# A ninth pair by seven products, one set of weight sums, and a fourth raw place in a hybrid encoder layer

## The chip, the core and the metric

The kernel runs on one core of a Trainium2 chip. A core has five engines with their own instruction queues: TensorE (PE, matrix products; PEld is its loading of the stationary operand), VectorE (DVE), ScalarE (ACT), GpSimd (POOL) and SyncE (SP), which here only issues the loads of weights. Each works through its queue in the order in which the program put the instructions there, and waits at an instruction until the semaphores that it names have come. The metric is the device time in microseconds of one execution of the program; the number given for a kernel is the median of several.

## The reference

One encoder layer on 256 frames of 4096 channels, all in float32. Cut to what matters:

```
h = layer_norm(x)                                   # 256 x 4096
proj = h @ w_in                                     # 4096 x 24592: sixteen thousand columns of
                                                    # q, k, v, g twice, 16 forget logits, 8192 gate logits
y_r = group_norm(retention(rotary(q_r), rotary(k_r), v_r)) * silu(g_r)
y_f = forgetting_attention(q_f, k_f, v_f, f_logit + b_forget) * silu(g_f)
gates = sigmoid(gate_logit + b_gate)
merged = gates[0] * (y_r @ w_branch_ret) + gates[1] * (y_f @ w_branch_fox)
out = layer_norm(2**0.25 * h + merged @ w_out)
```

The product `h @ w_in` is most of the work, and the change is in it alone.

## The kernel before

**Products in three parts.** Each float32 operand is split into a high part (a cast by ACT) and a low part (the operand minus the high part, by DVE), and one product is three matmuls: high by high, high by low, low by high (`three`, L199 to L202). `split_into` (L154) is the pair of instructions: line 155 is ACT's cast, line 156 DVE's subtraction. The rows of the profile name the tiles `whi` and `wlo` for weights, `hTh` and `hTl` for the transposed normalised input.

**Groups of sixteen pairs.** Most columns of `w_in` are worked off in groups of 1024 columns: four groups of gates and then sixteen of projections, twenty in all (L889 to L892). A group sums over 4096 input channels in sixteen *pairs* of 256 channels, in the order of `PAIRS` (L32): 8, 0, 9, 1, and so on to 15, 7. A pair is a 2 by 2 block product: two halves of 128 frames, two blocks of 128 channels, two halves of 512 columns.

**Plain pairs and seven pairs.** A plain pair does the eight block products in the obvious way, 24 matmuls of 128x512. A pair named in `SEVEN` (8 to 15, so eight of sixteen) does seven products of sums (the Winograd form of Strassen's scheme), 21 matmuls. For that it needs sums of blocks of the input, made once ahead of the first group (`make_sops`, L363, tiles `soh` and `sol`), and sums of blocks of the weights, made anew for every pair (`u_split`, L183 to L197): `ta` and `tb` in float32 by DVE, then cast and subtracted into the tile `tset`. `tset` holds t1 and t3 (from `ta`) and t2 and t4 (from `tb`). In what follows S is a seven pair, P a plain one, and S15 is the pair number 15.

**Banks.** A group's eight products are accumulated in the eight banks of PSUM: 1, 2, 6, 5 in the tiles `acc`, 3, 7, 4, x in the tiles `ps` (`pair_pe`, L219). A plain pair adds to 2, 3, 4 and x, a seven pair to all but x. Since all eight are in use, the next group can begin with a bank only when ACT has copied the old one out (`proj_evac`, L391, tiles `ev`): 1, 6, 5, 7 after the last seven pair, 2, 3, 4, x after the last pair. `combine` (L405) then makes the four output blocks out of the eight copies with DVE, eight additions for a projection and eleven for gates, one behind each of the next steps (`late_step`).

**What sets the order.** The places: raw weights come by DMA into `wraw` (1 MB for a pair), three places in turn (`RAW = 3`, `load_more`, L923, loads the next one when the splitting of an old one has been issued). The split weights of a pair go into one of two sets of tiles, the sets alternating from pair to pair (`slots_for`, L928); `tset` alternates between two places of its own, t0 and t1, which lie in the tiles `yb0` and `yb1` of the room that the input had. The order of the instructions in each engine's queue is then set by a scheduler in the tile framework, which moves instructions of neighbouring pairs past each other; nothing is moved while the kernel runs.

Of the kernel before, what the change touches and what calls it, by code (L numbers as in the profile page):

```python
# [8 lines left out]
F32 = mybir.dt.float32  # L9
F32R = mybir.dt.float32r  # L10
# [18 lines left out]
FRONT = 2  # L29
SEVEN = tuple(range(8, 16))  # L30
GATE0, GATE1 = 7, 15
PAIRS = tuple(p for i in range(8) for p in (8 + i, i))  # L32


@with_exitstack
def hybrid_kernel(
# [27 lines left out]
    def bcast(ap1, n0, n):  # L64
        return ap1[n0:n0 + n].rearrange("(o n) -> o n", o=1).to_broadcast([P, n])


    xt = []
    for t in range(T):
        xt.append(big.tile([P, D], F32, name=f"x{t}", tag=f"yb{t}"))  # L70
    for t in range(T):
# [52 lines left out]

    def add_pair(wname, hi, lo, sops, order, evac):

        holder = {}
        last = lambda some: max(i for i, p in enumerate(order) if (p in sops) == some)
        final = dict(x=last(False), **{k: last(True) for k in "1567"})
        for i, p in enumerate(order):  # L130
            loads.append(dict(n=4 * NC, srcs=[take(wname, 4 * P * NC)], users=1))
            units.append(dict(kind="p", ld=loads[-1], p=p, seven=p in sops, hi=hi, lo=lo, sops=sops, g=i,
                              ng=len(order), evac=evac, h=holder, drain=False, pre=None, final=final))

    def u_load(ld):
        raw = wp.tile([P, 4 * NC], F32, name="wraw", tag="wraw", bufs=RAW)
        w = ld["srcs"][0].shape[0] // P
        for i, src in enumerate(ld["srcs"]):
            nc.sync.dma_start(raw[:, i * w:(i + 1) * w], src.rearrange("(p f) -> p f", p=P))
        ld["raw"] = raw  # L140
# [18 lines left out]
    def u_split(u):  # L159
# [30 lines left out]
        split_into(st[1][0][:, :NC], st[1][1][:, :NC], B[3])  # L190
        ts = big.tile([P, 2, 2, 2, NC], F32R, name="tset", tag="yb0" if u["slots"][2] == "t0" else "yb1")
        for i, t_ in enumerate((ta, tb)):
# [26 lines left out]
    def pair_pe(u):  # L219
# [143 lines left out]
    def make_sops(hi, lo, pairs_, sops):  # L363
        sh = big.tile([P, len(pairs_), 4, P], F32R, name="soh", tag="yb2")
        sl = big.tile([P, len(pairs_), 4, P], F32R, name="sol", tag="yb3")
        for n_, p in enumerate(pairs_):
            sops[p] = (sh[:, n_], sl[:, n_])
        yield
        for n_, p in enumerate(pairs_):
# [8 lines left out]
            nc.vector.tensor_tensor(o[:, 0, :], a12, o[:, 2, :], op=ALU.add)  # L378
            split_into(sh[:, n_], sl[:, n_], o)
            yield  # L380
# [102 lines left out]
    def retention():  # L483
# [3 lines left out]
        yr["h"] = big.tile([P, 16, S], F32R, name="yrh", tag="yb0")  # L487
        yr["l"] = big.tile([P, 16, S], F32R, name="yrl", tag="yb1")

# [313 lines left out]
    def out_chunk(j):  # L803
# [3 lines left out]
        def pre():  # L807
            if not z:
                for t in range(T):
                    z[t] = big.tile([P, D], F32, name=f"z{t}", tag=f"yb{t}")  # L810
                bg.append(post_rows())
# [111 lines left out]
    def load_more():  # L923
        while state["loaded"] < min(len(loads), state["done"] + RAW):
            u_load(loads[state["loaded"]])
            state["loaded"] += 1

    def slots_for(i, s_):  # L928
        u = units[i]
        if u["kind"] == "p":  # L930
            cands = [("r0", "r1") if (i - first_pair) % 2 else ("a0", "a1")]
            if u["seven"]:
                state["t"] = state.get("t", 0)
                cands = [c + ("t" + str(state["t"] % 2),) for c in cands]
        else:
            cands = u["cands"]
        for c in cands:
            if all(q not in user or last_step[user[q]] < s_ for q in c):
                if u["kind"] == "p" and u["seven"]:
                    state["t"] += 1  # L940
                return c
        return None
# [52 lines left out]
    for s_, (i, tiles) in enumerate(steps):  # L995
# [140 lines left out]
```

## Time and profile before

| | |
|---|---|
| time, median of 3 runs | 2832.47 us (2830.31 to 2833.13) |
| the profiled execution | 2837.31 us, span 2835.5 us |
| PE busy | 2791.1 us, 98% |
| DVE busy | 2308.0 us, 81% |
| ACT busy | 1569.0 us, 55% |
| mean granted TensorE clock | 0.996 |

The four groups of gates lie at about 115 to 457 us of the span, the sixteen groups of projections at 457 to 1763 us, the attention branches, merge and output projection behind them. A busy time is the union of an engine's instructions. Durations of neighbours on one engine overlap by about a tenth of a microsecond, so the pace of an engine is read from start to start, not from the durations. The granted clock of 1.00 in a row is TensorE at 2.4 GHz, 0.50 would be 1.2 GHz throughout.

### The profile page before, as it was taken

What the parts mean: (1) busy time and instruction counts of PE and PEld (TensorE: products, weight loads), DVE (VectorE), ACT (ScalarE), POOL (GpSimd) and SP (SyncE); (2) the same over time, 40 slices, a digit from 0 to 9 for tenths busy, and PEclk for the clock granted to TensorE, in tenths of its full rate; (3) what the DMA queues carried; (4) which work ended last, traced back from release to release, by engine and by line L of the source; (5) the groups of instructions that cost most, each with busy time, mean ns of one, the idle gap of its engine ahead of it and who ended that gap; (6) DMA issues with size and microseconds to landing.
All of it is one profiled execution on the core that took longest, in us unless ns stands there. A gap on an engine that the chain in (4) does not pass through costs nothing. (4 is left out here: it accounts for less than half of the span.)

```text
span 2835.5 us, 34653 instructions
## 1 busy us (share of the span) xinstructions
PE 2791.1 (98%) x12666; PEld 2312.5 (82%) x12666; DVE 2308.0 (81%) x2988; ACT 1569.0 (55%) x2170; POOL 170.1 (6%) x302
## 2 busy tenths in 40 slices
PE   7999999999999999999999999999999999999998
PEld 5788888888888888888888888888898888888886
DVE  7889998999999999899999998977675666656666
ACT  5555666565566565655555565444664444444443
POOL 1000000000000000000000000212220000000000
PEclk9999999999999999999999999999999999999999
DMA  6456666656666655555665656866676556666564
GB/s 221 182 211 227 231 224 217 215 223 217 221 223 223 220 217 216 212 217 218 230 222 208 234 208 236 283 222 208 197 232 220 207 210 218 224 216 230 211 231 171
DMA packets 128157, 620.28 MB, mean 219 GB/s; under 512 B 15804, under 2 KB 16076, under 8 KB 87020
## 3 DMA queue, kind: packets, MB, share of 16 engines
q1 hardware_dynamic: 105552, 543.47, 53.2%
q0 software_dynamic: 21856, 72.49, 8.3%
q8 instruction: 99, 1.62, 0.2%
q10 hardware_dynamic: 576, 2.10, 0.2%
q14 instruction: 74, 0.60, 0.1%
HBM read 588.54 MB, written 29.46 MB: 218 GB/s over the span
## 5 line engine op out<-in xcount | busy, mean ns | idle before, releaser
L155 ACT CAST whi<-wraw 128x1024 fp32r<-128x1024 f32 (+1 forms) x640 | 594.5, 946 | 408.8 <-PE ps L202 221.5
L156 DVE TENSOR_TENSOR wpart<-wraw,wpart 128x512 fp32r<-128x512 f32 (+2 forms) x790 | 521.5, 669 | 316.0 <-ACT wpart L155 314.0
L155 ACT CAST wpart<-wraw 128x512 fp32r<-128x512 f32 (+2 forms) x790 | 475.4, 606 | 524.8 <-DVE wpart L156 312.9
L156 DVE TENSOR_TENSOR wlo<-wraw,whi 128x1024 fp32r<-128x1024 f32 (+1 forms) x640 | 684.4, 1088 | 23.2 <-ACT whi L155 23.0
L201 PE MATMUL ps<-wlo,hTh 128*128 128x512 f32 x960 | 374.5, 390 | 0.6 <-DVE wlo L156 0.6
L202 PE MATMUL ps<-whi,hTl 128*128 128x512 f32 x960 | 374.4, 390 | 0.0
L200 PE MATMUL ps<-whi,hTh 128*128 128x512 f32 x960 | 328.3, 390 | 0.0
L186 DVE TENSOR_TENSOR ta<-wraw 128x1024 f32<-128x1024 f32 x160 | 195.9, 1225 | 113.2 <-DMA wraw<-in_w_in 112.5
L201 PE MATMUL acc<-wlo,hTh 128*128 128x512 f32 x640 | 246.9, 390 | 4.2 <-DVE wlo L156 4.1
L200 PE MATMUL acc<-whi,hTh 128*128 128x512 f32 x640 | 246.3, 390 | 1.5 <-ACT whi L155 1.4
L202 PE MATMUL acc<-whi,hTl 128*128 128x512 f32 x640 | 246.1, 389 | 0.0
L155 ACT CAST tset<-tb 128x1024 fp32r<-128x1024 f32 x160 | 168.5, 1053 | 129.1 <-DVE tb L189 128.7
L155 ACT CAST tset<-ta 128x1024 fp32r<-128x1024 f32 x160 | 168.1, 1051 | 119.8 <-DVE ta L186 119.6
L201 PE MATMUL acc<-wpart,hTh 128*128 128x512 f32 (+2 forms) x568 | 212.1, 377 | 4.1 <-DVE wpart L156 4.1
L201 PEld LDWEIGHTS ps<-wlo,hTh 128*128 128x128 f32 x960 | 180.6, 188 | 38.6 <-DVE wlo L156 1.0
L200 PEld LDWEIGHTS ps<-whi,hTh 128*128 128x128 f32 x960 | 180.7, 188 | 37.7
L202 PEld LDWEIGHTS ps<-whi,hTl 128*128 128x128 f32 x960 | 180.7, 188 | 37.6
L202 PE MATMUL acc<-wpart,hTl 128*128 128x512 f32 (+2 forms) x568 | 208.6, 371 | 0.6 <-DVE rstd L96 0.6
L156 DVE TENSOR_TENSOR tset<-tb,tset 128x1024 fp32r<-128x1024 f32 x160 | 195.5, 1222 | 1.1 <-ACT tset L155 1.1
L156 DVE TENSOR_TENSOR tset<-ta,tset 128x1024 fp32r<-128x1024 f32 x160 | 195.4, 1221 | 0.0
L201 PE MATMUL acc<-wpart,mTh 128*128 128x512 f32 x500 | 194.6, 389 | 0.0
L202 PE MATMUL acc<-wpart,mTl 128*128 128x512 f32 x500 | 194.5, 389 | 0.0
(257 smaller groups left out, 4853.8 us busy)
## 6 DMA issues: line engine op xcount, KB each, us to landing
wraw<-in_w_in SPq DMA_DIRECT2D x320, 1024.0 KB, 4.9
wraw<-in_w_out SPq DMA_DIRECT2D x128, 512.0 KB, 4.1
wraw<-in_w_in SPq DMA_DIRECT2D x112, 512.0 KB, 4.5
wraw<-in_w_branch_ret SPq DMA_DIRECT2D x64, 512.0 KB, 4.2
wraw<-in_w_branch_fox SPq DMA_DIRECT2D x64, 512.0 KB, 4.2
proj_d<-ev POOLq DMA_DIRECT2D x64, 256.0 KB, 2.7
g<-gates_d POOLq DMA_DIRECT2D x16, 512.0 KB, 5.7
wraw<-in_w_in SPq DMA_DIRECT2D x16, 272.0 KB, 4.3
```

The costliest lines, as they stand in the source:

```text
L155: c = nc.scalar.copy(hi, src)
L156: nc.vector.tensor_tensor(lo, src, hi.bitcast(F32), op=ALU.subtract)
L186: nc.vector.tensor_tensor(ta, B[0][:, None, :].to_broadcast([P, 2, NC]), raw[:, NC:3 * NC].rearrange("p (a n) -> p a n", a=2), op=ALU.add)
L200: nc.tensor.matmul(o, lhsT=a[0], rhs=w[0], start=first, stop=False)
L201: nc.tensor.matmul(o, lhsT=a[0], rhs=w[1], start=False, stop=False)
L202: return nc.tensor.matmul(o, lhsT=a[1], rhs=w[0], start=False, stop=last)
```

## The change

Nine of the sixteen pairs go by seven products in the sixteen groups of projections (7 to 15); in the four groups of gates pair 7 stays plain. The order of pairs becomes 8, 0, 9, 1, 10, 2, 11, 3, 12, 4, 13, 5, 14, 7, 15, 6, so that in a projection S14, S7 and S15 follow one another. There is one `tset` instead of two. Its second room and a part of the room of the sums of the input become: a fourth place for raw weights, `wraw3`, which takes every fourth pair's load, and the ninth pair's sums of the input (`sope`). The loads may run four pairs ahead. The products of a seven pair and the copies of the banks come in another order, those with t1 and t3 first. The tile `x1`, `yrl` and `z1`, which lie in the same room later or earlier, are kept in two halves.

```diff
-SEVEN = tuple(range(8, 16))
+SEVEN = tuple(range(7, 16))
-PAIRS = tuple(p for i in range(8) for p in (8 + i, i))
+PAIRS = (8, 0, 9, 1, 10, 2, 11, 3, 12, 4, 13, 5, 14, 7, 15, 6)
...
     def u_load(ld):
-        raw = wp.tile([P, 4 * NC], F32, name="wraw", tag="wraw", bufs=RAW)
+        if ld.get("pair", 0) % 4 == 3:
+            raw = scr["raw"]
+        else:
+            raw = wp.tile([P, 4 * NC], F32, name="wraw", tag="wraw", bufs=RAW)
...
-        ts = big.tile([P, 2, 2, 2, NC], F32R, name="tset", tag="yb0" if u["slots"][2] == "t0" else "yb1")
+        ts = scr["t"]
...
-            work_ = [("1", blk(0, 0), f["b11"]), ("6", so(2), f["t2"]), ("5", so(1), f["t1"]), ("7", so(3), f["t3"]),
-                     ("2", blk(0, 1), f["b21"]), ("3", so(0), f["b22"]), ("4", blk(1, 1), f["t4"])]
+            work_ = [("5", so(1), f["t1"]), ("7", so(3), f["t3"]), ("6", so(2), f["t2"]), ("1", blk(0, 0), f["b11"]),
+                     ("4", blk(1, 1), f["t4"]), ("2", blk(0, 1), f["b21"]), ("3", so(0), f["b22"])]
...
     def make_sops(hi, lo, pairs_, sops):
-        sh = big.tile([P, len(pairs_), 4, P], F32R, name="soh", tag="yb2")
-        sl = big.tile([P, len(pairs_), 4, P], F32R, name="sol", tag="yb3")
+        so = [big.tile([P, 4, 2, 4, P], F32R, name="sop", tag=f"yb{2 + i}") for i in range(2)]
+        end = big.tile([P, 2, 2, 4, P], F32R, name="sope", tag="yb1b")
+        scr["t"] = big.tile([P, 2, 2, 2, NC], F32R, name="tset", tag="yb0")
+        scr["raw"] = big.tile([P, 4 * NC], F32, name="wraw3", tag="yb1a")
...
     for i in range((GATE1 - GATE0) // 2):
-        add_pair("w_in", hTh, hTl, sops, PAIRS, proj_evac(gates[GATE0 + 2 * i][0], True))
+        add_pair("w_in", hTh, hTl, sops, PAIRS, proj_evac(gates[GATE0 + 2 * i][0], True), 7)
...
     def load_more():
-        while state["loaded"] < min(len(loads), state["done"] + RAW):
+        while state["loaded"] < len(loads):
+            pair = loads[state["loaded"]].get("pair", 0)
+            if state["loaded"] >= state["done"] + RAW + (pair >= RAW and "raw" in scr) or pair == RAW and "raw" not in scr:
+                break
             u_load(loads[state["loaded"]])
...
-            u["evac"](u["h"]["m"], "1657")
+            u["evac"](u["h"]["m"], "5761")
         if u["g"] == u["ng"] - 1:
             if u["kind"] == "p":
-                u["evac"](u["h"]["m"], "234x")
+                u["evac"](u["h"]["m"], "423x")
```

The change moves instructions most at the end of each group of projections. The sixteen ends have two orders that alternate, eight of the one, seven of the other; the last end is followed by other work. Below is what stands there. In the changed file the cast is line 182, the subtraction 183, the matmuls of `three` 227 to 229, the bank copies 430.

ACT's queue at the end of the sixth group of projections, before. `acc_6865` to `ps_6872` are the banks 1, 2, 6, 5, 3, 7, 4, x in this order, `tset_7452` and `whi_7441`, `whi_7439` belong to the next group's first pair:

```order
L155 CAST tset_7452<-ta_7445 128x1024
L155 CAST whi_7402<-wraw_7299 128x1024
L400 COPY ev_7431<-acc_6865 128x512
L400 COPY ev_7433<-acc_6867 128x512
L400 COPY ev_7435<-acc_6868 128x512
L400 COPY ev_7437<-ps_6870 128x512
L155 CAST whi_7441<-wraw_7333 128x512
L155 CAST whi_7439<-wraw_7333 128x1024
L155 CAST tset_7452<-tb_7446 128x1024
L155 CAST whi_7491<-wraw_7374 128x1024
L400 COPY ev_7483<-acc_6866 128x512
L400 COPY ev_7485<-ps_6869 128x512
```

The same place of the changed kernel, an end of the second order. `acc_6800` to `ps_6807` are the banks in the order above; `ta_7318` and `tb_7319` are the sums of S15, `ta_7375` and `tb_7376` of the next group's S8:

```order
L182 CAST tset_798<-ta_7318 128x1024
L430 COPY ev_7418<-ps_6807 128x512
L182 CAST tset_798<-tb_7319 128x1024
L430 COPY ev_7361<-acc_6803 128x512
L430 COPY ev_7363<-ps_6805 128x512
L182 CAST tset_798<-ta_7375 128x1024
L430 COPY ev_7365<-acc_6802 128x512
L182 CAST whi_7420<-wraw_7289 128x1024
L430 COPY ev_7412<-ps_6806 128x512
L430 COPY ev_7414<-acc_6801 128x512
L182 CAST tset_798<-tb_7376 128x1024
L430 COPY ev_7416<-ps_6804 128x512
```

Before, the first four copies stand ahead of the next group's casts and the last four together behind them; now the copy of bank x stands ahead of the cast of S15's own t2 and t4, and seven of the eight copies stand among the casts of two pairs.

ACT's queue at the end before that one, of the first order; `tset_798` is written from S8's `ta_6745` and `tb_6746`, `whi_6790` is pair 0 of the next group:

```order
L430 COPY ev_6788<-ps_6177 128x512
L430 COPY ev_6731<-acc_6173 128x512
L430 COPY ev_6733<-ps_6175 128x512
L182 CAST tset_798<-ta_6745 128x1024
L430 COPY ev_6735<-acc_6172 128x512
L182 CAST tset_798<-tb_6746 128x1024
L182 CAST whi_6790<-wraw_6659 128x1024
L430 COPY ev_6782<-ps_6176 128x512
L430 COPY ev_6784<-acc_6171 128x512
L430 COPY ev_6786<-ps_6174 128x512
```

Here seven copies and three casts stand in a row between bank x and bank 3, where before four copies did.

TensorE's queue at the same end (second order), before, from the last matmuls of the plain pair 7 into the next group (`acc_7501`, `acc_7503`, `acc_7504` are its banks 1, 6, 5):

```order
L201 MATMUL acc_6866<-wlo_7403,hTh_109 128x512
L202 MATMUL acc_6866<-whi_7402,hTl_110 128x512
L201 MATMUL ps_6869<-wlo_7403,hTh_109 128x512
L202 MATMUL ps_6869<-whi_7402,hTl_110 128x512
L201 MATMUL ps_6871<-wlo_7403,hTh_109 128x512
L202 MATMUL ps_6871<-whi_7402,hTl_110 128x512
L201 MATMUL ps_6872<-wlo_7403,hTh_109 128x512
L202 MATMUL ps_6872<-whi_7402,hTl_110 128x512
L200 MATMUL acc_7501<-whi_7439,hTh_109 128x512
L200 MATMUL acc_7503<-tset_7452,soh_794 128x512
L200 MATMUL acc_7504<-tset_7452,soh_794 128x512
L201 MATMUL acc_7504<-tset_7452,soh_794 128x512
```

And after, from the last matmul of bank x (`ps_6807`) on; `sope_797` are the sums of the input of S15, and a matmul of line 228 reads the low part that DVE writes:

```order
L229 MATMUL ps_6807<-whi_7333,hTl_111 128x512
L227 MATMUL acc_6803<-tset_798,sope_797 128x512
L227 MATMUL ps_6805<-tset_798,sope_797 128x512
L228 MATMUL acc_6803<-tset_798,sope_797 128x512
L229 MATMUL acc_6803<-tset_798,sope_797 128x512
L228 MATMUL ps_6805<-tset_798,sope_797 128x512
L229 MATMUL ps_6805<-tset_798,sope_797 128x512
L227 MATMUL acc_6802<-tset_798,sope_797 128x512
L227 MATMUL ps_6806<-tset_798,hTh_110 128x512
L228 MATMUL acc_6802<-tset_798,sope_797 128x512
L229 MATMUL acc_6802<-tset_798,sope_797 128x512
L228 MATMUL ps_6806<-tset_798,hTh_110 128x512
```

Before, a group ends with plain work on banks 2, 3, 4, x; now the products of S15 with the sums of the weights have slid behind most of the plain pair 6, and bank x is done ahead of them.

## Rows read from the trace of the kernel before

**Rows 1.** The page, span and part 1: busy us of each engine, share, instructions.

```profile
span 2835.5 us, 34653 instructions
...
PE 2791.1 (98%) x12666; PEld 2312.5 (82%) x12666; DVE 2308.0 (81%) x2988; ACT 1569.0 (55%) x2170; POOL 170.1 (6%) x302
```

**Rows 2.** Stretches: us, then busy us (instructions) by engine, granted clock, DMA, GB/s.

```profile
100.00:200.00 100.00, 94.87 (x397) 75.97 (x396) 86.76 (x119) 56.21 (x67) 0.75 (x1) 0.97 0.51 185
200.00:500.00 300.00, 297.84 (x1304) 243.55 (x1303) 277.99 (x305) 183.40 (x222) 12.47 (x23) 1.00 0.64 225
500.00:1700.00 1200.00, 1200.00 (x5295) 993.63 (x5295) 1100.39 (x1179) 715.61 (x828) 31.91 (x59) 1.00 0.61 219
```

**Rows 3.** Timeline of DVE inside a projection group: start, duration, instruction.

```profile
1000.81 1.22 DVE L156 TENSOR_TENSOR wlo<-wraw,whi 128x1024 fp32r<-128x1024 f32 x1
...
1001.95 0.69 DVE L188 TENSOR_TENSOR tb<-ta,wraw 128x512 f32<-128x512 f32 x1
...
1002.55 1.22 DVE L156 TENSOR_TENSOR tset<-ta,tset 128x1024 fp32r<-128x1024 f32 x1
```

**Rows 4.** DVE by line and shape, 500 to 1600 us: count, busy us, mean ns.

```profile
L156 DVE TENSOR_TENSOR wlo<-wraw,whi 128x1024 fp32r<-128x1024 f32 x325 | 397.1, 1222 | 14.3 <-ACT whi L155 14.1
L186 DVE TENSOR_TENSOR ta<-wraw 128x1024 f32<-128x1024 f32 x108 | 132.3, 1225 | 77.7 <-DMA wraw<-in_w_in 77.1
L156 DVE TENSOR_TENSOR tset<-tb,tset 128x1024 fp32r<-128x1024 f32 x108 | 131.9, 1222 | 0.0
...
L156 DVE TENSOR_TENSOR wlo<-wraw,whi 128x512 fp32r<-128x512 f32 x108 | 74.4, 689 | 0.0
...
L420 DVE TENSOR_TENSOR ev<-ev 128x512 f32<-128x512 f32 x104 | 69.4, 690 | 0.0
```

**Rows 5.** Timeline at the end of a projection group, PE and ACT.

```profile
1030.44 0.39 PE L202 MATMUL acc<-whi,hTl 128*128 128x512 f32 x1
...
1030.87 0.59 ACT L400 COPY ev<-acc 128x512 f32<-128x512 f32 x1 [0.26 <-PE acc L202]
...
1031.36 1.57 ACT L400 COPY ev<-ps 128x512 f32<-128x512 f32 x3
...
1032.79 1.08 ACT L155 CAST whi<-wraw 128x1024 fp32r<-128x1024 f32 x1
...
1033.74 1.07 ACT L155 CAST tset<-ta 128x1024 fp32r<-128x1024 f32 x1
```

**Rows 6.** Timeline behind a group of gates: DVE, ACT and the waiting PE.

```profile
233.96 1.23 DVE L156 TENSOR_TENSOR wlo<-wraw,whi 128x1024 fp32r<-128x1024 f32 x1
...
235.04 0.62 ACT L155 CAST whi<-wraw 128x512 fp32r<-128x512 f32 x1 [1.71 <-DMA wraw<-in_w_in]
...
235.25 0.50 PE L201 MATMUL acc<-wlo,hTh 128*128 128x512 f32 x1
```

**Rows 7.** Waits, 500 to 1600 us: total us, times, longest.

```profile
ACT whi L155 <- PE ps L202: 147.6, 94, 3.7
...
DVE ta L186 <- DMA wraw<-in_w_in: 77.1, 66, 3.4
```

**Rows 8.** Timeline of PE, first group of gates, around idle time.

```profile
137.88 0.62 PE L200 MATMUL ps<-whi,hTh 128*128 128x512 f32 x2
141.27 0.50 PE L201 MATMUL acc<-wlo,hTh 128*128 128x512 f32 x1 [2.77 <-DVE wlo L156]
...
142.24 0.63 PE L201 MATMUL ps<-wlo,hTh 128*128 128x512 f32 x1
...
145.22 0.43 PE L200 MATMUL ps<-tset,hTh 128*128 128x512 f32 x1
```

**Rows 9.** DVE by line and shape, 90 to 135 us: the sums of the input.

```profile
L372 DVE TENSOR_TENSOR sv<-hTh,hTl 128x512 f32<-128x512 f32 x8 | 5.4, 673 | 0.0
L156 DVE TENSOR_TENSOR sol<-so,soh 128x512 fp32r<-128x512 f32 x8 | 5.4, 672 | 0.0
...
L377 DVE SCALAR_TENSOR_TENSOR so<-so,sv 128x128 f32<-128x128 f32 x8 | 2.2, 273 | 0.0
```

More of the change, by code (lines that the diff above doesn't have):

```diff
@@ L65, in bcast, with __init__, __getitem__, big1 @@
         return ap1[n0:n0 + n].rearrange("(o n) -> o n", o=1).to_broadcast([P, n])
+    class Halves:
+        def __init__(self, a, b, half):
+            self.t, self.half = (a, b), half
+        def __getitem__(self, key):
+            p, c, *rest = key
+            h = self.half
+            if isinstance(c, slice):
+                i = c.start // h
+                c = slice(c.start - i * h, c.stop - i * h)
+            else:
+                i, c = divmod(c, h)
+            return self.t[i][(p, c, *rest)]
+    def big1(shape, dt, name):
+        half = [P, shape[1] // 2] + shape[2:]
+        return Halves(*[big.tile(half, dt, name=name + e, tag="yb1" + e) for e in "ab"], shape[1] // 2)
     xt = []
     for t in range(T):
-        xt.append(big.tile([P, D], F32, name=f"x{t}", tag=f"yb{t}"))
+        xt.append(big1([P, D], F32, "x1") if t else big.tile([P, D], F32, name="x0", tag="yb0"))
     for t in range(T):
@@ L123, in add_chunk, with add_pair @@
                               cands=(cands if cands and g < 2 else [("r0",), ("r1",)])))
-    def add_pair(wname, hi, lo, sops, order, evac):
+    npairs = [0]
+    def add_pair(wname, hi, lo, sops, order, evac, plain=None):
         holder = {}
-        last = lambda some: max(i for i, p in enumerate(order) if (p in sops) == some)
+        last = lambda some: max(i for i, p in enumerate(order) if (p in sops and p != plain) == some)
         final = dict(x=last(False), **{k: last(True) for k in "1567"})
         for i, p in enumerate(order):
-            loads.append(dict(n=4 * NC, srcs=[take(wname, 4 * P * NC)], users=1))
-            units.append(dict(kind="p", ld=loads[-1], p=p, seven=p in sops, hi=hi, lo=lo, sops=sops, g=i,
+            loads.append(dict(n=4 * NC, srcs=[take(wname, 4 * P * NC)], users=1, pair=npairs[0]))
+            npairs[0] += 1
+            units.append(dict(kind="p", ld=loads[-1], p=p, seven=p in sops and p != plain, hi=hi, lo=lo, sops=sops, g=i,
                               ng=len(order), evac=evac, h=holder, drain=False, pre=None, final=final))
+    scr = {}
     def u_load(ld):
-        raw = wp.tile([P, 4 * NC], F32, name="wraw", tag="wraw", bufs=RAW)
+        if ld.get("pair", 0) % 4 == 3:
+            raw = scr["raw"]
+        else:
+            raw = wp.tile([P, 4 * NC], F32, name="wraw", tag="wraw", bufs=RAW)
         w = ld["srcs"][0].shape[0] // P
@@ L363, in make_sops @@
     def make_sops(hi, lo, pairs_, sops):
-        sh = big.tile([P, len(pairs_), 4, P], F32R, name="soh", tag="yb2")
-        sl = big.tile([P, len(pairs_), 4, P], F32R, name="sol", tag="yb3")
+        so = [big.tile([P, 4, 2, 4, P], F32R, name="sop", tag=f"yb{2 + i}") for i in range(2)]
+        end = big.tile([P, 2, 2, 4, P], F32R, name="sope", tag="yb1b")
+        scr["t"] = big.tile([P, 2, 2, 2, NC], F32R, name="tset", tag="yb0")
+        scr["raw"] = big.tile([P, 4 * NC], F32, name="wraw3", tag="yb1a")
         for n_, p in enumerate(pairs_):
-            sops[p] = (sh[:, n_], sl[:, n_])
+            hl = so[n_ // 4][:, n_ % 4] if n_ < 8 else end[:, 0]
+            sops[p] = (hl[:, 0], hl[:, 1])
         yield
@@ L378, in make_sops @@
             nc.vector.tensor_tensor(o[:, 0, :], a12, o[:, 2, :], op=ALU.add)
-            split_into(sh[:, n_], sl[:, n_], o)
+            split_into(*sops[p], o)
             yield
@@ L487, in retention @@
         yr["h"] = big.tile([P, 16, S], F32R, name="yrh", tag="yb0")
-        yr["l"] = big.tile([P, 16, S], F32R, name="yrl", tag="yb1")
+        yr["l"] = big1([P, 16, S], F32R, "yrl")
         def fetch_qk(gi):
@@ L809, in pre @@
                 for t in range(T):
-                    z[t] = big.tile([P, D], F32, name=f"z{t}", tag=f"yb{t}")
+                    z[t] = big1([P, D], F32, "z1") if t else big.tile([P, D], F32, name="z0", tag="yb0")
                 bg.append(post_rows())
@@ L932, in slots_for @@
             if u["seven"]:
-                state["t"] = state.get("t", 0)
-                cands = [c + ("t" + str(state["t"] % 2),) for c in cands]
+                cands = [c + ("t",) for c in cands]
         else:
@@ L938, in slots_for @@
             if all(q not in user or last_step[user[q]] < s_ for q in c):
-                if u["kind"] == "p" and u["seven"]:
-                    state["t"] += 1
                 return c
```

## The prediction

> **What bounds the kernel now.** Start with the page: PE is busy for 98% of the span and DVE for 81% [rows 1]. Such shares mix stages, so the next view is the busy time by stretch [rows 2]. From 500 to 1700 us, inside the projections, PE is busy for all of 1200 us and ran 5295 matmuls: one every 226.6 ns, at a granted clock of 1.00, 2.4 GHz. A group of eight seven pairs and eight plain ones is 8 x 21 + 8 x 24 = 360 matmuls, 81.6 us. Nothing but the number of matmuls counts there. From 200 to 500 us, in the gates, 300 us have room for 1324 matmuls and 1304 ran: 20 places, 4.5 us, were lost. From 100 to 200 us there is room for 441 and 397 ran: 44 places, 10 us. So the two places where something other than PE decides are the first group and the ends of the groups of gates.
>
> The second engine is DVE, busy for 1100.4 of the 1200 us, 92% [rows 2]. Its pace is read from start to start [rows 3]: a subtraction over 1024 columns begins 1.14 us ahead of the next instruction, one over 512 columns 0.60 us, although the durations are 1.22 and 0.69. The columns of counts [rows 4] show that all its work in this stage is of these two sizes. Its waits are 77 us for raw weights [rows 4, 7], but PE never waited: DVE ran ahead and was held back. The change spends that reserve, so the question is whether it is enough at every point of a group.
>
> **The matmuls removed.** In each of the sixteen projections one pair goes from 24 to 21 matmuls: 48 x 226.6 ns = 10.9 us less. The Trainium skill, page "TensorE: Matmul & The Clock Gate", section "Back-to-back issue gap", gives about 131 ns for a sustained stream of matmuls of 512 columns; by that the saving would be 6.3 us. The trace has 226.6 ns here, and that decides.
>
> **DVE's work added.** A seven pair costs DVE four long instructions (the low part of two blocks, ta, twice tset) and three short ones (the low part of a third block, twice tb): 4 x 1.14 + 3 x 0.60 = 6.36 us. A plain pair costs 2 x 1.14 = 2.28. The combination of a group's blocks is eight short ones, 4.8 us. Before: 8 x 6.36 + 8 x 2.28 + 4.8 = 73.9 of 81.6 us, 91%, which agrees with the 92% read. After: 9 x 6.36 + 7 x 2.28 + 4.8 = 78.0 of 357 x 0.2266 = 80.9 us, 96%. On the average PE stays the bound, with 2.9 us of DVE to spare per group. But S14, S7 and S15 now stand in a row: 19.1 us of DVE beside 63 matmuls, 14.3 us. The missing 4.8 us must come out of DVE's lead, and the lead is bounded: a pair's tiles are those of the pair two before it, and the one tset is free only when PE has used the old one.
>
> **The ends of the projections, step by step.** I set zero at the first matmul of S14, and take it that DVE is as far ahead as the tiles allow; PE's place in its queue times 0.2266 is when it is due. Handing over takes 0.04 us from the end of a matmul to ACT (1030.83 to 1030.87), and 0.06 from DVE to PE (235.19 to 235.25) [rows 5, 6]. A copy of a bank keeps ACT for 0.48 us (three from 1031.36 to 1032.79), a long cast 0.95 (1032.79 to 1033.74), 1.07 to its end [rows 5].
>
> Second order (seven ends). S7's tiles are P5's, so DVE begins S7's low parts one cast after zero, at 1.3. Nine long and seven short instructions bring it to the end of S15's tb: 1.3 + 10.3 + 4.2 = 15.8. Bank x's last matmul is 68 places on: due at 15.41, over at 15.80. ACT copies x from 15.84 to 16.32, and only then casts S15's tb, to 17.38; DVE subtracts from 17.42, to 18.64; PE could go on at 18.70. That matmul is 77 places on, due at 17.45. PE stands for 1.25 us. Had the cast stood ahead of the copy it would have been no earlier than 15.8, so the copy costs 0.5 and DVE's lateness 0.75. Behind it I followed the next group to its fifth pair: DVE is 0.5 to 4 us ahead of each matmul.
>
> First order (eight ends). Bank x is over 70 places on, at 16.25; ACT's row from there is x, 5, 7, a cast, 6, two casts, 4, 2, 3. The last copy begins after six copies and three casts, 16.29 + 2.88 + 2.85 = 22.02, and ends 0.6 later; PE needs bank 3 at its place 98, due at 22.21. It stands for about 0.5 us. Before, PE did not stand at all at these ends, as only four copies stand in ACT's row [rows 2, 5].
>
> Together 8 x 0.5 + 7 x 1.25 = 12.8 us. Its bounds: nothing, as before, if DVE and ACT are a little quicker than I reckon; and 2.25 us at each of fifteen ends, 34 us, if DVE comes 1 us later than the tiles allow (a wait for raw weights is 77.1 / 66 = 1.2 us in the mean [rows 7]). I take 12.8: each step of it has a row.
>
> **The gates and the fourth place.** There pair 7 stays plain and S and P alternate; copies and casts keep a tidy order. Behind their ends ACT waited for raw weights, 1.71 us in the row shown, DVE and then PE behind it [rows 6]. A fourth place lets a load start a pair earlier, some 5 us. I take 4.0 of the 4.5 us lost there as won. Bounds: 4.5 won; 5 lost, if the single tset makes four ends stand for 1.25 us as above. That tset has only one place costs nothing between S and P by the trace: a plain pair, 24 matmuls or 5.4 us, covers a cast and a subtraction, 2.3 us.
>
> **The front.** The ninth pair's sums of the input are two short DVE instructions and four of 128 columns (0.2 us from start to start), 2 x 0.60 + 4 x 0.20 = 2.0 us [rows 9], in a stretch where DVE is what PE waits for; against it, pair 3's weights are loaded ahead of the first group, and the stand up to 141.27, 2.77 us and then half clock [rows 8], came when loads were late. Bounds 3.4 us more (2.0 and once the 1.4 of the clock below) and 3.4 less; I take 0. The halves of x1, yrl and z1 change no instruction's size. The same bytes are loaded.
>
> **Sum.** -10.9 + 12.8 - 4.0 + 0 = -2.1 us. Made against the profiled execution, 2837.3 us (a span of 2835.5 and 1.8 around it), it gives 2835.2. That execution is 4.8 us above the median; the same difference from the median of 2832.5 gives **2830.4 us**: no change that can be told, since about 0.2%, 5.7 us, is what a measurement of this kernel can tell.
>
> **Rivals.** *The ends cost little.* If DVE and ACT are on time the 10.9 and 4.0 us stay: 2832.5 - 14.9 = 2817.6; with half of the stands, 2824. For it: PE was not once late in 1200 us before, and my chain has margins of tenths. Against: the copies and casts do stand in one row, and a copy's 0.48 us is measured.
>
> *The clock falls at the ends.* After PE had stood for 2.77 us the granted clock fell to its lower level, 1.2 GHz: seven matmuls from 142.24 to 145.22 took 2.98 us instead of 1.59, 1.4 us more [rows 8]. If a stand of 1.25 us is enough for that, seven ends add 9.8 us: 2840.2, slower than before; with the eight short stands too, 2851. It decides from the point where one stand brings on a fall. Against it: I see no fall behind stands this short in the rows, and 200 to 500 us shows 1.00 despite 4.5 us lost in several stands [rows 2]. The Trainium skill, page "TensorE: Matmul & The Clock Gate", section "A second HAM failure mode: psum-queue depth-cycling", says that brief idling between groups of matmuls that wait for banks can make the clock swing between its levels. By that rule the time is this rival's.
>
> *DVE lacks the lead.* If raw weights or the one tset keep DVE 1 us short of what the tiles allow, fifteen ends stand 1 us longer: 2845.4. For it: a reserve of 2.9 us in 80.9. Against: four places take most of the waits for raw weights away.
>
> *The fourth place does nothing*, and the gates stay as they are: 2834.4, still no change.
>
> **Chances.** Forecast, with the idle fourth place, 0.45 (its own range 2827 to 2838); little cost at the ends 0.30; the clock 0.10; DVE short 0.15. So faster by over 0.2% 0.30, within 0.2% 0.45, slower 0.25. The range of 8 in 10 goes from the first rival's 2818 to the last's 2846.
>
> **What will show it.** In 500 to 1700 us: about 55 places of 226.6 ns fewer than PE has room for, in PE waits for DVE's tset or wlo and for ACT's copies, at intervals of a group, nothing in between; the copy of bank x ahead of a tset cast in every second end. DVE near 96%, its waits for raw weights small. In 200 to 500 us nearly no lost place. I am wrong on the ends if PE is at 100% in the projections; on the lead if PE also waits in the middle of groups; on the clock if it shows below 0.99 there.

## The result

The changed kernel takes 2848.35 us (median of four runs, 2846.8 to 2849.9), the kernel before, run beside it, 2832.06. The ratio is 1.0056 (95% interval 1.0044 to 1.0068): slower by 0.56%, 12 to 19 us by the interval. Forecast were 2830.4 us and no change that can be told, with a range up to 2846; the result lies outside it.

The profiled execution took 2846.80 us, against 2837.31 of the one before. First the page's busy times of the changed kernel, then its stretches (length; for each engine busy us and count; last the granted clock, DMA share and GB/s); they answer to [rows 1, 2].

```profile
PE 2787.3 (98%) x12618; PEld 2300.7 (81%) x12618; DVE 2377.1 (84%) x3074; ACT 1595.5 (56%) x2203; POOL 170.7 (6%) x302
```

```profile
100.00:200.00 100.00, 93.77 (x399) 75.16 (x398) 93.87 (x132) 56.58 (x68) 0.75 (x1) 0.98 0.53 195
200.00:500.00 300.00, 300.00 (x1325) 248.51 (x1324) 281.50 (x307) 190.55 (x226) 12.48 (x23) 1.00 0.64 227
500.00:1700.00 1200.00, 1186.21 (x5196) 971.89 (x5195) 1145.62 (x1235) 728.37 (x848) 30.83 (x57) 1.00 0.60 216
```

In the gates (200 to 500 us) PE is full, as forecast. In the projections it ran 5196 matmuls where 5296 had room: 100 places, 22.7 us, where I forecast 55. DVE is busy for 95.5%, the forecast 96. Its waits for raw weights [rows 7] are gone. The waits of PE from 500 to 1700 us, with the sum, the count and the longest:

```profile
PE acc L227 <- ACT tset L182: 10.1, 21, 1.0
PE acc L228 <- DVE tset L183: 3.7, 7, 0.5
```

These sums fall short of 22.7 us, because a matmul's end is modelled and hides part of each stand. Start to start is the better measure. The following rows of PE are the places from 540 to 623 us where clearly more than 0.2266 us lie between two starts: first one in the middle of a group, then those at an end of the second order, each with the row ahead of it (start, duration, operation, and in brackets the idle time and who ended it; the first row stands for two matmuls).

```profile
571.72 0.61 PE L227 MATMUL ps<-whi,hTh 128*128 128x512 f32 x2
572.50 0.50 PE L227 MATMUL acc<-tset,sop 128*128 128x512 f32 x1 [0.16 <-ACT tset L182]
572.84 0.39 PE L227 MATMUL ps<-tset,hTh 128*128 128x512 f32 x1
...
615.25 0.39 PE L229 MATMUL ps<-tset,sope 128*128 128x512 f32 x1
615.90 0.50 PE L227 MATMUL acc<-tset,sope 128*128 128x512 f32 x1 [0.26 <-ACT tset L182]
616.23 0.40 PE L227 MATMUL ps<-tset,hTh 128*128 128x512 f32 x1
617.16 0.50 PE L228 MATMUL acc<-tset,sope 128*128 128x512 f32 x1 [0.53 <-DVE tset L183]
617.50 0.39 PE L229 MATMUL acc<-tset,sope 128*128 128x512 f32 x1
...
620.70 0.39 PE L229 MATMUL ps<-tset,sop 128*128 128x512 f32 x1
622.10 0.50 PE L227 MATMUL acc<-tset,sop 128*128 128x512 f32 x1 [1.01 <-ACT tset L182]
622.44 0.40 PE L227 MATMUL acc<-whi,hTh 128*128 128x512 f32 x1
```

The first matmul behind a stand takes 0.34 us instead of 0.23, so each stand costs 0.11 more than its gap. At the second-order end S15's products of t2 and t4 come 0.53 and 0.81 us late, together 1.34 (forecast 1.25), by the chain that was forecast: bank x is copied ahead of the cast of S15's tb, and DVE's subtraction waits for that cast.

```profile
614.31 0.59 ACT L430 COPY ev<-ps 128x512 f32<-128x512 f32 x1 [3.89 <-PE ps L229]
614.80 1.05 ACT L182 CAST tset<-tb 128x1024 fp32r<-128x1024 f32 x1
```

```profile
615.88 1.23 DVE L183 TENSOR_TENSOR tset<-tb,tset 128x1024 fp32r<-128x1024 f32 x1 [1.02 <-ACT tset L182]
```

Then there is a stand that the forecast did not have: 1.17 + 0.11 = 1.28 us at 622.10, the first product of the next group's S8 with t2. It comes back every 165.07 us (622.10, 787.17, 952.21); two groups without a stand are 714 x 0.2266 = 161.8 us. So a group loses 1.63 us, 24 to 26 us over the projections.

At the first-order ends, for which 0.5 us was forecast, PE does not stand: over the end at 528 to 545 us it loses less than 0.1 us. The copy of bank 3 is as late as forecast, but PE begins that bank's product on time, inside the copy's recorded time:

```profile
539.04 0.63 ACT L430 COPY ev<-ps 128x512 f32<-128x512 f32 x1
539.31 0.39 PE L227 MATMUL ps<-whi,sop 128*128 128x512 f32 x1
```

The 0.44 us at 572.50 are another stand: 156 matmuls behind the group's first product with sums and 201 ahead of the next group's, over 30 us from any copy of a bank, and in every second group. It too is a product with t2 that waits for ACT's cast of the second sums. DVE had that sum ready at 570.30; the cast stood behind three casts of raw weights, the first of which waited for PE:

```profile
568.97 2.53 ACT L182 CAST whi<-wraw 128x1024 fp32r<-128x1024 f32 x3 [0.53 <-PE ps L229]
571.40 1.04 ACT L182 CAST tset<-tb 128x1024 fp32r<-128x1024 f32 x1
```

```profile
569.62 0.68 DVE L216 TENSOR_TENSOR tb<-tb,wraw 128x512 f32<-128x512 f32 x1
```

The stand at 622.10 is read from ACT's and DVE's rows ahead of it in the same way:

```profile
617.93 0.59 ACT L430 COPY ev<-acc 128x512 f32<-128x512 f32 x1 [0.17 <-PE acc L229]
619.09 1.06 ACT L182 CAST whi<-wraw 128x1024 fp32r<-128x1024 f32 x1 [0.57 <-PE ps L229]
620.05 0.57 ACT L430 COPY ev<-ps 128x512 f32<-128x512 f32 x1
620.52 0.58 ACT L430 COPY ev<-acc 128x512 f32<-128x512 f32 x1
621.00 1.05 ACT L182 CAST tset<-tb 128x1024 fp32r<-128x1024 f32 x1
```

```profile
618.94 0.68 DVE L216 TENSOR_TENSOR tb<-tb,wraw 128x512 f32<-128x512 f32 x1
```

DVE had S8's sums ready at 619.62. The cast that PE needs (`tset<-tb`, 621.00) stands in ACT's queue behind the cast of the next plain pair, which itself waited 0.57 us for PE to give its tile free, and behind two copies of banks. PE was due at 620.93 and started at 622.10.

### The profile page after: what moved, and what is told of

It is laid out like the page before. It is cut to its first block, busy times and chain, and to the rows that moved or that the text cites. A ratio compares the mean times of both kernels' runs of the same rounds, so it can differ in the third digit from the quotient of the medians.

```text
span 2845.0 us, 35025 instructions
## 1 busy us (share of the span) xinstructions
PE 2787.3 (98%) x12618; PEld 2300.7 (81%) x12618; DVE 2377.1 (84%) x3074; ACT 1595.5 (56%) x2203; POOL 170.7 (6%) x302
## 5 line engine op out<-in xcount | busy, mean ns | idle before, releaser
L228 PE MATMUL ps<-wlo,hTh 128*128 128x512 f32 x864 | 336.4, 389 | 0.0
L229 PE MATMUL ps<-whi,hTl 128*128 128x512 f32 x864 | 334.4, 389 | 0.0
L182 ACT CAST tset<-tb 128x1024 fp32r<-128x1024 f32 x176 | 185.4, 1053 | 82.4 <-PE ps L229 67.0
L183 DVE TENSOR_TENSOR tset<-tb,tset 128x1024 fp32r<-128x1024 f32 x176 | 214.4, 1218 | 16.0 <-ACT tset L182 15.9
L183 DVE TENSOR_TENSOR tset<-ta,tset 128x1024 fp32r<-128x1024 f32 x176 | 214.3, 1217 | 6.9 <-ACT tset L182 6.0
L228 PE MATMUL acc<-wpart,hTh 128*128 128x512 f32 (+2 forms) x568 | 212.8, 378 | 4.5 <-DVE wpart L183 4.4
L213 DVE TENSOR_TENSOR ta<-wraw 128x1024 f32<-128x1024 f32 x176 | 214.2, 1217 | 0.7
L182 ACT CAST tset<-ta 128x1024 fp32r<-128x1024 f32 x176 | 185.3, 1053 | 25.1 <-PE ps L229 15.0
L227 PEld LDWEIGHTS ps<-whi,hTh 128*128 128x128 f32 x864 | 162.5, 188 | 34.1 <-ACT whi L182 0.3
L227 PE MATMUL acc<-wpart,hTh 128*128 128x512 f32 (+2 forms) x568 | 186.1, 379 | 3.8 <-ACT wpart L182 3.6
L228 PEld LDWEIGHTS ps<-wlo,hTh 128*128 128x128 f32 x864 | 162.4, 188 | 33.9
```

Of the source, the lines that this page charges most:

```text
L182: c = nc.scalar.copy(hi, src)
L183: nc.vector.tensor_tensor(lo, src, hi.bitcast(F32), op=ALU.subtract)
L213: nc.vector.tensor_tensor(ta, B[0][:, None, :].to_broadcast([P, 2, NC]), raw[:, NC:3 * NC].rearrange("p (a n) -> p a n", a=2), op=ALU.add)
L227: nc.tensor.matmul(o, lhsT=a[0], rhs=w[0], start=first, stop=False)
L228: nc.tensor.matmul(o, lhsT=a[0], rhs=w[1], start=False, stop=False)
L229: return nc.tensor.matmul(o, lhsT=a[1], rhs=w[0], start=False, stop=last)
```

## The experiments

Two theories to begin with. A: the place of casts in ACT's queue at the ends decides. B: DVE has no time left. The edits are given in short, on the changed kernel. In kernels with more lines the line numbers are shifted by a few.

**castfirst.** The casts of the second sums ahead of the copies x, 4, 2, 3 and of the next plain pair's casts:

```
+ u["tbc"] = split_into(ts[:, i, 0], ts[:, i, 1], t_)
- u["evac"](u["h"]["m"], "423x")
+ with issue_after(tbc of this S15, tbc of the next S8):
+     u["evac"](u["h"]["m"], "x423")
...
+ with tc.issue_after(units[i - 1]["tbc"]):   # at a group's second pair
      u_split(u)
```

> Edit of the changed kernel: at each group's end ACT casts the seven pairs' second sums (tset<-tb of S15 and of the next group's S8) ahead of the bank copies x, 4, 2, 3 and of the next plain pair's casts. Theory A (ACT's row at the ends: casts that PE needs stand behind copies and behind a cast that waits for a slot): of the 1.6 us that each of the 16 projections lost in the mean, the 1.2 us behind the next group's product 6 and the 0.5 us for the copy of x in every second end go, 10 to 13 us in all: 2835 to 2838 us. Theory B (DVE has no time left, 78.0 of 80.9 us by the estimate): DVE's work is the same, so 2846 to 2850.

Measured 2838.68 us, 1.0028 (1.0017 to 1.0039) of before: 9.7 less than the changed kernel, a little above A's range. But by the profile only about 4 of them are in the projections: the period fell from 82.53 to 82.29 us per group. The rest is mostly 16 matmuls more from 100 to 200 us, of which below. With the cast ahead of the copies, ACT waits for DVE at a second-order end:

```profile
694.93 0.59 ACT L430 COPY ev<-acc 128x512 f32<-128x512 f32 x1
697.01 1.05 ACT L182 CAST tset<-tb 128x1024 fp32r<-128x1024 f32 x1 [1.48 <-DVE tb L216]
```

PE starts there only 0.16 us late, where it was 1.17, but every end now has this order, the first-order ends too, where PE did not stand before, and S9's first cast stands behind the copies instead. Neither theory alone says that.

**nocomb.** DVE's eight additions of the combination are left out of the projections.

```
+ if gate:
      nc.vector.tensor_tensor(v[o], v[x], v[y], op=how)
```

> Edit of the changed kernel: in the sixteen projections the combination of the group's blocks (eight additions of 512 columns on DVE, 4.8 us per group) is left out; ACT's copies and the stores stay. Theory A (ACT's row at the ends): only DVE's own lateness at the second-order ends, 7 x 0.75 = 5 us, can go: 2842 to 2849. Theory B (DVE has no time left): DVE falls to 73.2 of 80.9 us per group, the share it had before, and the stands go, 26 us: 2822 to 2826.

Measured 2820.11 us, 0.996 (0.9947 to 0.9972): every stand is gone, PE ran 5292 of 5296 matmuls. That is 2 us below B's range. But with a lighter DVE the scheduler had also set the cast of S8's sums ahead of P0's cast and the two copies, as ACT's row of this run shows:

```profile
617.47 1.08 ACT L182 CAST tset<-tb 128x1024 fp32r<-128x1024 f32 x1
618.42 1.08 ACT L182 CAST whi<-wraw 128x1024 fp32r<-128x1024 f32 x1
619.37 0.61 ACT L430 COPY ev<-ps 128x512 f32<-128x512 f32 x1
```

So the run changed two things, and the next one separates them.

**nocomb_late.** The same, with that cast put back behind them at every end, one copy later than in the changed kernel (the subtraction that goes with the cast moves along):

```
+ split_into(ts[:, 0, 0], ts[:, 0, 1], ta)
+ u["rest"] = lambda: split_into(ts[:, 1, 0], ts[:, 1, 1], tb)
...
+ with issue_after(copy of bank 2), issue_after(cast of P0):
+     units[i + 1].pop("rest")()
```

> The changed kernel with the combination's additions left out of the projections as in nocomb, and with ACT's cast of the next group's second sums (tset<-tb8) put behind the copies of banks 4, 2 and 3 and behind the next plain pair's cast, as it stands in the changed kernel and one copy later still; in nocomb the scheduler had put it ahead of them. So DVE has its time, and ACT the bad order. Theory A (ACT's row): PE stands 1.2 us or more behind it at least at every second end, 8 x 1.2 = 10 us above nocomb's 2820: 2830 or more. Theory B (DVE's time alone): 2820 to 2822 as nocomb.

Measured 2849.84 us, 1.0064 (1.005 to 1.0078): 29.7 us above nocomb with the same work. DVE's sum, ACT's row and PE in this run:

```profile
619.93 0.69 DVE L217 TENSOR_TENSOR tb<-tb,wraw 128x512 f32<-128x512 f32 x1
```

```profile
621.87 1.05 ACT L182 CAST whi<-wraw 128x1024 fp32r<-128x1024 f32 x1
622.84 0.57 ACT L433 COPY ev<-ps 128x512 f32<-128x512 f32 x1
623.31 0.59 ACT L433 COPY ev<-acc 128x512 f32<-128x512 f32 x1
623.79 0.60 ACT L433 COPY ev<-ps 128x512 f32<-128x512 f32 x1
624.26 1.07 ACT L182 CAST tset<-tb 128x1024 fp32r<-128x1024 f32 x1
```

```profile
623.55 0.40 PE L232 MATMUL ps<-tset,sop 128*128 128x512 f32 x1
625.38 0.50 PE L230 MATMUL acc<-tset,sop 128*128 128x512 f32 x1 [1.43 <-ACT tset L182]
```

The sum lay ready for 3.6 us. The place in the row is enough by itself for a stand of 1.6 us at every end, with DVE's load as light as in nocomb. So A is shown as a cause, and B as the only cause has fallen.

**spread.** Another order of pairs in the projections; no three seven pairs in a row:

```
+ SPREAD = (8, 0, 9, 10, 1, 11, 2, 12, 3, 13, 14, 4, 15, 5, 7, 6)
```

> Edit of the changed kernel: the projections take their pairs in the order 8, 0, 9, 10, 1, 11, 2, 12, 3, 13, 14, 4, 15, 5, 7, 6, so that two seven pairs stand together in two places in the middle of a group and never three, and a group ends S P S P as before the change. Theory A (three seven pairs in a row push casts into the row of copies): PE no longer stands at the ends, 26 us less: 2822 to 2826 us. Theory B (DVE's time): the load of DVE is the same 96%, stands come at the doubled pairs instead: 2838 to 2848.

Measured 2832.0 us, 1.0003 (0.9995 to 1.0012). Neither figure. The ends stand nowhere, but once in each group, at a doubled pair, PE is late; the period is 81.57 us, 0.67 above 80.90. DVE's work is the same as in the changed kernel, so 15 of the 26 us hang on the order of pairs, and on the rows that the scheduler made of it, and not on the amount of DVE's work.

```profile
638.69 0.49 PE L228 MATMUL acc<-tset,sop 128*128 128x512 f32 x1 [0.34 <-ACT tset L183]
```

**spread_casts.** Since this cast too stood behind other casts, each seven pair's second cast goes ahead of all casts of the pair behind it:

```
- with tc.issue_after(units[i - 1]["tbc"]):   # at a group's second pair
+ with tc.issue_after(units[i - 1]["tbc"]):   # at every pair
      u_split(u)
```

> The order of pairs of spread (8, 0, 9, 10, 1, 11, 2, 12, 3, 13, 14, 4, 15, 5, 7, 6 in the projections), and in ACT's row the cast of every seven pair's second sums (tset<-tb) ahead of the casts of the pair behind it and of the copies x, 4, 2, 3. In spread PE stood once in each group, 0.67 us by the period of 81.57 us against 357 x 0.2266 = 80.90, and the cast it waited for stood behind two casts of the next pair. Theory A (the place of that cast in ACT's row): the stand goes, period 80.9, 10.8 us less than spread's 2832.0: 2821, and with what castfirst won from 100 to 200 us 2818. Theory B (DVE's 96%): another stand takes its place, 2828 to 2834.

Measured 2849.28 us, 1.0066 (1.0052 to 1.008): the opposite of A's figure. ACT's row, then PE:

```profile
635.87 1.57 ACT L183 CAST whi<-wraw 128x1024 fp32r<-128x1024 f32 x2 [4.34 <-PE ps L230]
637.34 1.04 ACT L183 CAST tset<-tb 128x1024 fp32r<-128x1024 f32 x1
```

```profile
637.03 0.45 PE L228 MATMUL acc<-whi,hTh 128*128 128x512 f32 x1
638.44 0.50 PE L228 MATMUL acc<-tset,sop 128*128 128x512 f32 x1 [0.96 <-ACT tset L183]
```

The two long casts of the plain pair did go behind the needed one (to 638.29). But two other casts stand right ahead of it, as in spread; they now wait 4.34 us for PE, and the needed one waits behind them. A cast that moves forward in a queue starts earlier only if what still stands ahead of it starts early.

**spread_casts_g9.** The same, nine seven pairs also in the gates.

```
- add_pair("w_in", hTh, hTl, sops, PAIRS, proj_evac(gates[GATE0 + 2 * i][0], True), 7)
+ add_pair("w_in", hTh, hTl, sops, SPREAD, proj_evac(gates[GATE0 + 2 * i][0], True))
```

> As spread_casts, and the four groups of gates take nine seven pairs in the same order too: 12 matmuls less, 2.7 us. The combination of a group of gates has three more additions on DVE, 1.8 us per group, so DVE's load there is 79.8 of 80.9 us. If the gates hold: 2.7 us below spread_casts. If DVE's load makes them stand at the four ends by 1 us or more: the same as spread_casts, or up to 4 us above.

Measured 2859.29 us, 1.0098 (1.0084 to 1.0112), 10 above spread_casts: the gates, with three more additions per group, now lose 67 places from 200 to 500 us (1258 matmuls of 1325). Worse than the worst I allowed.

**ten.** As spread_casts with ten seven pairs.

```
+ SEVEN = tuple(range(6, 16))
+ SPREAD = (8, 0, 9, 10, 1, 11, 12, 2, 13, 3, 14, 15, 4, 7, 6, 5)
```

> As spread_casts with ten seven pairs in the projections (6 to 15; 8, 0, 9, 10, 1, 11, 12, 2, 13, 3, 14, 15, 4, 7, 6, 5), pairs 6 and 7 plain in the gates: 354 matmuls, 80.2 us, per projection; DVE 10 x 6.36 + 6 x 2.28 + 4.8 = 82.1 us. If DVE's time by that sum is the bound, a group takes 82.1 us or a little more, 1.2 us more than at spread_casts' best: 2838 to 2845. If DVE were not yet the bound at ten: 80.2 us, 2807 to 2810.

Measured 2888.12 us, 1.0201 (1.0187 to 1.0215). The direction is right, the size not: a group takes 84.9 us, not 82.1. With DVE at 97% (1166.77 of 1200 us) PE stood 39 times for ACT's tset casts, ACT itself waiting 247 us for DVE's tb.

**poolcomb and pool_castfirst.** The additions moved to GpSimd, without and with castfirst's edit:

```
- nc.vector.tensor_tensor(v[o], v[x], v[y], op=how)
+ (nc.vector if gate else nc.gpsimd).tensor_tensor(v[o], v[x], v[y], op=how)
```

> The changed kernel with the eight additions of each projection's combination moved from DVE to GpSimd, all the work done. DVE's load falls to 73.2 of 80.9 us per group as in nocomb. If GpSimd's work disturbs nobody: 2820 to 2823 us, faster than before by the 48 matmuls, 10.9 us. If GpSimd and DVE slow each other while both work, DVE's subtractions behind a group's end become longer and stands come back: 2826 to 2848. No trace here shows an addition of 512 columns on GpSimd yet.

> The changed kernel with both edits: the combination's additions on GpSimd, and ACT's casts of the second sums ahead of the copies at the ends, as in castfirst, which also ran 16 matmuls more than the changed kernel from 100 to 200 us (3.6 us). If that gain at the front stays and the ends stand nowhere: 2817 us. If the front's gain was that one execution's: 2820. If GpSimd disturbs DVE: 2826 or more.

Measured 2917.55 us, 1.0302 (1.0288 to 1.0316), and 2939.74, 1.0382 (1.0368 to 1.0396): the first far outside the ranges that I wrote, the second inside only because "2826 or more" has no upper end. The two engines slow each other. One addition on GpSimd and DVE's work beside it, in poolcomb:

```profile
625.68 1.37 POOL L450 TENSOR_TENSOR ev<-ev 128x512 f32<-128x512 f32 x1 [70.11 <-ACT ev L430]
...
627.92 7.01 POOL L450 TENSOR_TENSOR ev<-ev 128x512 f32<-128x512 f32 x4
```

```profile
625.80 2.33 DVE L183 TENSOR_TENSOR wlo<-wraw,whi 128x1024 fp32r<-128x1024 f32 x1
628.05 1.79 DVE L215 TENSOR_TENSOR tb<-ta,wraw 128x512 f32<-128x512 f32 x1
```

DVE's subtraction takes 2.33 instead of 1.22 us, its short addition 1.79 instead of 0.69: each 1.1 us longer. The Trainium skill, page "SBUF — State Buffer", section "SBUF: two separate sides", says that a DVE operation with two inputs in SBUF and a GpSimd operation that reads SBUF exclude each other for a whole instruction; the trace agrees, as far as it shows this: 1.1 us more per DVE instruction, for the long and the short ones alike.

**two_tb and two_tb_spread.** The fourth raw place's room becomes a second place for the half of `tset` made from tb; the second with spread's order:

```
+ scr["t2"] = big.tile([P, 2, 2, NC], F32R, name="tseb", tag="yb1a")
...
+ tsb = scr["t2"] if state["t"] % 2 else ts[:, 1]
```

> The changed kernel with the room of the fourth place for raw weights given to a second place for the half of tset that is made from tb (three raw places as before the change). The order of casts and copies in ACT's row at the ends stays what it is in the changed kernel. If the one tset is what makes the casts late (a cast of S8's second sums can start only when PE has read those of S15), the stands at the second-order ends go: 2830 to 2836. If the place of the cast in ACT's row decides, whatever the room: 2845 to 2851.

> The pair order of spread with the second place for the tb half instead of the fourth raw place. If the one tset keeps the doubled pairs' cast late in spread (0.67 us per group): 2821 to 2824. If the row decides: 2830 to 2834 as spread.

two_tb: 2848.41 us, 1.0058 (1.0046 to 1.0071), as the changed kernel, with the same stand to the hundredth:

```profile
624.15 0.50 PE L229 MATMUL acc<-tseb,sop 128*128 128x512 f32 x1 [1.02 <-ACT tseb L182]
```

With a second place the cast need not wait until PE has read S15's half, but it stands behind the same cast and copies in the row. So the one tset is not the cause of this stand. two_tb_spread: 2870.03 us, 1.0133 (1.0119 to 1.0147), missed on both counts: with three raw places this order waits for weights, in ACT first (5.49 us at 652.50).

**before_again, eight, eight_three.** What the fourth raw place is worth: the kernel before again; the changed kernel with pair 7 plain everywhere; and that with three raw places.

```
- add_pair("w_in", hTh, hTl, sops, PAIRS, proj_evac(2 * i * NC))
+ add_pair("w_in", hTh, hTl, sops, PAIRS, proj_evac(2 * i * NC), 7)   # eight, eight_three
- if ld.get("pair", 0) % 4 == 3:
+ if False:                                                           # eight_three
```

> The kernel before once more, for a second profile of it. In the first profile PE lost 20 places (4.5 us) from 200 to 500 us, and that execution took 2837.3 us against a median of 2832; the kernel with eight pairs and a fourth place for raw weights loses none there and still takes 2832.2. If the loss at the gates belongs to that one execution (loads that came late), a second profile shows 1320 or more matmuls from 200 to 500 us, and the fourth place has nothing to win. If it is in every execution, it shows 1304 again, and the eight-pair kernel loses its 4 us elsewhere.

> Edit of the changed kernel: pair 7 stays plain in the projections too (eight pairs by seven products, 48 matmuls more), with the fourth place for raw weights, the one tset and the new order of products and copies kept. Theory A and B both say that the projections run without a stand as before, and the gates keep their 4.5 us: 2827 to 2829 us. If one tset costs something by itself between alternating pairs: 2832 or more.

> The kernel eight (eight pairs by seven products, one tset, the new order of products and copies) with three places for raw weights. The second profile of the kernel before lost only 3 or 4 places at the gates, so the fourth place should be worth nothing that can be told: 2830 to 2834, as eight (2832.2). If the fourth place wins the 4 us that one profile showed: 2835 to 2838.

Measured 2831.24 (0.9999, 0.9989 to 1.001), 2832.17 (1.0001, 0.9992 to 1.0011) and 2832.2 (0.9999, 0.999 to 1.0008): no difference anywhere. The stretch 200 to 500 us of the first and the last; eight ran 1325 matmuls there too:

```profile
200.00:500.00 300.00, 299.42 (x1321) 247.57 (x1320) 281.35 (x308) 187.27 (x225) 12.46 (x23) 1.00 0.65 228
```

```profile
200.00:500.00 300.00, 300.00 (x1325) 248.52 (x1324) 282.50 (x308) 191.18 (x227) 12.48 (x23) 1.00 0.65 226
```

The second profile of the kernel before lost 4 places there, not the 20 of the first [rows 2]: the first was that one execution. The fourth place wins nothing with eight pairs. eight also shows that one tset and the new orders cost nothing there (in the projections it has all 5296 matmuls).

**spread_castfirst.** spread with castfirst's edit (at the groups' ends alone).

> spread and castfirst together: at the groups' ends the casts of the second sums ahead of the copies and of the next plain pair's casts only (not ahead of every pair's casts, as in spread_casts). In spread the ends stand nowhere, so the edit changes little in the projections: 10.8 us of stands remain. If castfirst's 16 matmuls more from 100 to 200 us come back: 2828 to 2829; if not: 2831 to 2833.

Measured 2828.86 us, 0.9987 (0.9978 to 0.9996): the one version below both kernels, 0.13% below the one before, as expected. The projections are spread's (5251 matmuls against 5252), and from 100 to 200 us there are 415 instead of 399. The rows behind that: in the changed kernel PE stood 3.34 us in the first group of pairs, in this one 1.07.

```profile
126.66 0.64 PE L227 MATMUL acc<-tset,sop 128*128 128x512 f32 x1 [3.34 <-ACT tset L182]
127.10 0.63 PE L227 MATMUL ps<-tset,hTh 128*128 128x512 f32 x1
```

```profile
123.49 0.50 PE L228 MATMUL acc<-tset,sop 128*128 128x512 f32 x1 [1.07 <-ACT tset L183]
```

Behind the longer stand the clock was at its lower level, 1.2 GHz: eight matmuls from 126.66 on start 0.43 us apart instead of 0.23 (granted clock 0.69 from 125 to 130 us). That is some 1.6 of the 3.6 us; in spread_castfirst the clock stayed at 1.00 there.

## Why the prediction was wrong

- *The matmuls removed, -10.9 us*: right. nocomb, which has no stand, is 11.5 us below the kernel before.
- *DVE's load of 96%*: right, 95.5% measured. The doubt whether that is enough was right too, though it acts through ACT.
- *The ends of the projections, +12.8 us*: this step failed. 24 to 26 us were measured. Of its terms one was right, in its chain and in its size: S15's own products at the second-order ends (1.34 for 1.25). The sentence that failed is "Behind it I followed the next group to its fifth pair: DVE is 0.5 to 4 us ahead of each matmul". DVE was ahead, but I had checked DVE and the copies of the banks there and not the cast in ACT: the high part for S8's first t2 product stood behind two copies and a cast that waits for PE. That is 1.28 us at each second-order end, some 9 us, which the forecast had at nothing.
- *The first-order ends, 8 x 0.5 us of that*: wrong too. PE lost less than 0.1 us there, not 0.5: I let PE wait for the recorded end of the last bank's copy, and it didn't. About the same sum, 0.44 us in every second group, was lost in the middle of groups, again for a cast of second sums behind casts that wait for PE. That the size agrees is luck. I had expected "nothing in between", and had named waits in the middle of groups as a sign against DVE's lead; here DVE's sum lay ready 1.1 us before the cast.
- *The gates and the fourth place, -4.0 us*: failed as well. The profile to profile count bears it out (1325 for 1304 matmuls), the medians don't: the 20 places lost belonged to the one profiled execution, which was 4.8 us above its median. I noted that difference and carried it through as a constant instead of asking in which row it lay; it lay in the very row from which I took the gain.
- *The front, 0*: right, 399 matmuls from 100 to 200 us against 397 and 400 in the two profiles of the kernel before.
- The sum with what was measured: -10.9 + 25 + 0 = 14 us on the median of 2832, 2846, against 2848.35. The 2 us left are within the interval, 3 us to either side. By the profiles about as much lies in the work just behind the projections, where PE's stands for weights come to 3.6 us (1790 to 1813 us) against 1.7 in the second profile of the kernel before.
- *The rivals.* The clock did not fall: 1.00 through the projections with several stands of 0.4 to 1.3 us in two groups, so the rule cited there from the Trainium skill ("TensorE: Matmul & The Clock Gate", section "A second HAM failure mode: psum-queue depth-cycling") is not what this trace shows. In the first group the runs differ: behind stands of 1.4 and 1.25 us, 2.3 us apart, the clock fell in castfirst (0.72 from 125 to 130 us) and did not in spread_castfirst (1.00); what decides that stays open. "DVE lacks the lead" was nearest by its figure, 2845.4, but not by its reason: neither raw weights (no such wait is left) nor the one tset (two_tb has the same stand) made PE stand at 622.10, and DVE's sum was there in time. "The ends cost little" is what nocomb shows for a DVE with time to spare.

What stays open: why the scheduler sets the rows as it does. Each run that changed DVE's load or the order of pairs got another row, so an edit's own cost and that of the new row could be told apart only where the row was forced, as in nocomb_late. The stand in the middle of groups was read from rows alone; no run moved that cast by itself. What let PE begin bank 3's product at 539.31, inside the recorded time of its copy, the rows don't show.

## What to carry to other kernels

When two engines feed a third, follow every operand of each matmul to its own engine: each product here needs a cast from ACT and a difference from DVE, and a lead on one says nothing of the other. What stands ahead of an instruction in an in-order queue, and what that waits for, can cost more than the instruction's own time; and a helper engine with 4% to spare needs its order right to the single instruction. A loss read from one profile is a loss of that execution until a second profile shows it. And a term that comes out at its forecast size is confirmed only when the rows show it at its forecast place.

## Not expected of the hardware

- GpSimd's addition of 512 columns takes 1.37 us where it comes first (twice DVE's 0.69), 1.75 in a row beside DVE, and makes each DVE instruction beside it 1.1 us longer, so moving 4.8 us of work per group off DVE cost 97 us in all against nocomb, where that work is left out.
- Each stand of PE in the projections, of 0.1 to 1.6 us alike, costs 0.11 us more: the first matmul behind it takes 0.34 us to the next start instead of 0.23.
